# A gMLP and SwiGLU layer on one core: wd's operands prepared in quarters that share a ring with the input product, one k a step

## The chip, the cores and the metric

One Trainium2 chip, one of its cores. The metric is device time in microseconds (us) of one execution; the kernel before takes 1915.26 us, the median of three runs (1911.7 to 1916.3).

## The reference, cut to what matters

One post-norm layer on 2048 tokens of width 1024: a gated MLP mixer with spatial mixing, a layer norm, then a SwiGLU feed-forward part, with shift, scale and gate of both parts computed from a conditioning vector c. All data are float32.

```python
mod = silu(c) @ mod_w + mod_b
sh1, sc1, g1, sh2, sc2, g2 = split(mod, 6)
y = gmlp_mixer(x * (1 + sc1) + sh1)
x = layer_norm(ALPHA * x + (1 + g1) * y) * ln1_g + ln1_b
h = x * (1 + sc2) + sh2
g, u = split(h @ ffn_w_in, 2)          # 1024 -> 2 x 2816
y = (silu(g) * u) @ ffn_w_out          # 2816 -> 1024; ffn_w_out is the kernel's wd
out = layer_norm(ALPHA * x + (1 + g2) * y) * ln2_g + ln2_b
```

## The kernel before, in words

Each float32 product is three TensorE products: `parts` (line 91) splits an operand of 128 x 512 into a rounded part (a cast on ACT, line 94) and the rest (a subtraction on DVE, line 95). Both products of the feed-forward part use a Strassen-Winograd scheme: seven products of sums of blocks in place of eight. `A_OF` and `B_OF` name the operands of the seven.

The program first does the mixer for four blocks of 512 tokens (`v_part`, `us_part`, `y_part`), then `ffn_in` (line 451) twice, once for each half of the tokens (sb 0 and 1), then `ffn_out` (line 600).

`ffn_in` runs over eleven steps fp = 0..10. In a step the products stand in the order 1, 2, 5, 6, 7, 4, 3, each for the gate and the up weights (names f_<fp>g and f_<fp>u): 14 groups of 12 matmuls into the banks X, Y and Z of PSUM. `weight` (line 464) loads the four blocks of wf for product 1 (two loads of 512 KB for each of g and u), forms the sums of the later products in place on POOL (line 86), and splits each; it is called four products ahead of the matmuls. Banks are copied to SBUF tiles of the ring `c` on ACT (lines 498, 506, 513) and added to on DVE (lines 502, 514, 519); after the seven products come SiLU and product (lines 524 to 528). The seven results g, u and a21 of a step are all tiles of that ring, which has eight slots of 128 x 512. `a_operands` (line 427) forms four sums on POOL, and seven stores (line 530) bring the operands of the next product to HBM (aop).

`wd_prep(k)` (line 535) prepares wd's operands for k = 0..10: two loads of 128 x 1024 rows of wd (line 545, tiles of the ring `h3`, four slots of 128 x 1024), two multiplications by the gate g2 on DVE (line 548), four differences on DVE (line 555: T1, T3, T2, T4), and seven stores to HBM (line 540: B11, B21, B22 and the four T), which `ffn_out` reads back. g2's row comes from `spread` (line 144), called at step (5, 3) of the first half. The pieces of the eleven k are handed to the second half's steps by the table at line 768, which names steps 3 to 10 of it; `h3` serves in the same half for the loads of the half's own operands (`load_ops`, line 437). All loads and stores are issued in order on SP's queue.

The order in the source is not the order of the engines: a scheduler with a simulated clock sets the order of the instructions on each engine, and places an instruction as early as its tile's slot, its operands and its engine are free in that simulation. So the pieces of wd_prep, named for steps 3 to 10 of the second half, stand on the engines from step 0 to step 3 of it.

```python
for k, fp in enumerate((3, 4, 4, 5, 6, 6, 7, 8, 8, 9, 10)):
    for pr, step in zip((1, 2, 5, 6, 7, 4, 3), wd_prep(k)):
        later.setdefault((fp, pr), []).append(step)
```

Of the kernel before, what the change touches and what calls it, by code (L numbers as in the profile page):

```python
# [11 lines left out]
ALU = mybir.AluOpType  # L12

P = 128
# [23 lines left out]
def gmlp_swiglu_layer(  # L38
# [13 lines left out]
    nc = tc.nc  # L52
# [11 lines left out]
    ROW, HALF, UNIT = ([P, D], F32), ([P, 512], F32), ([P, 2, 512], F32R)  # L64
    cur, n = {}, [0]

    def phase(side, **tags):

        st = ExitStack()
        for tag, (bufs, kind) in tags.items():  # L70
            n[0] += 1
            p = st.enter_context(tc.tile_pool(name=f"{tag}{n[0]}", bufs=bufs, side=side, reuse_waits="tile"))
            cur[tag] = (p, kind)
        return st

    def new(tag, name, kind=None):
        p, (shape, dt) = cur[tag][0], kind or cur[tag][1]
        return p.tile(shape, dt, tag=tag, name=name)

    lo, hi = slice(0, 512), slice(512, 1024)  # L80
# [63 lines left out]
    def spread(k, name, tag="late"):  # L144

        line = dram.tile([ND, P], F32, name=f"{name}_line")
        nc.sync.dma_start(out=line.rearrange("d p -> p d"), in_=modc[:, k * ND : (k + 1) * ND])
        t = new(tag, name)
        nc.sync.dma_start(out=t, in_=line.rearrange("d p -> (d p)").partition_broadcast(P))
        return t  # L150
# [106 lines left out]
    sh1, sc1, g1, sh2, sc2, g2 = ([None] * ND for _ in range(6))  # L257
    env = {}
# [178 lines left out]
    def load_ops(sb, names):  # L437
        def tag_of(n, k):

            return "late" if n in ("A22", "S3") or (n == "S4" and k > 1) else "ops" + n  # L440

        out = {}
        for n in names:
            out[n] = []
            for k in range(NK):
                t = new("h3" if sb else "s" if n in ("S3", "A22") else "hr", f"h2{n}r_{sb}_{k}", HALF)
                nc.sync.dma_start(out=t, in_=hop[A_AT[n]][k][sb])
                out[n].append(parts(t, f"h2{n}_{sb}_{k}", tag_of(n, k)))
        return out
# [85 lines left out]
    def wd_prep(k):  # L535

        w = []

        def store(n, src):
            nc.sync.dma_start(out=wdt[n][k], in_=src)  # L540

        def load():
            for q in range(2):
                w.append(new("h3", f"wd{k}_{q}", ROW))
                nc.sync.dma_start(out=w[q], in_=wd[(2 * k + q) * P : (2 * k + q + 1) * P, :])

        def scale(q):
            nc.vector.tensor_tensor(out=w[q], in0=w[q], in1=env["g2"], op=ALU.mult)
            for n, cs in ((("B11", lo),), (("B21", lo), ("B22", hi)))[q]:
                store(n, w[q][:, cs])  # L550

        def total(n):
            b11, b12, b21, b22 = w[0][:, lo], w[0][:, hi], w[1][:, lo], w[1][:, hi]
            o, a, b = {"T1": (b11, b12, b11), "T3": (b12, b22, b12), "T2": (b22, b22, b11), "T4": (b21, b21, b22)}[n]
            nc.vector.tensor_tensor(out=o, in0=a, in1=b, op=ALU.subtract)
            store(n, o)

        return [load, lambda: scale(0), lambda: scale(1)] + [lambda n=n: total(n) for n in ("T1", "T3", "T2", "T4")]
# [153 lines left out]
    for b in range(NB):  # L712
# [35 lines left out]
    env["mix"].close()  # L748
    mix.close()
    rest = phase(  # L750
        "left", s=(4, HALF), opsS4=(2, UNIT), opsS2=(4, UNIT), h3=(4, ROW), c=(8, HALF), w=(6, UNIT), opsS1=(4, UNIT), g2=(1, ROW),
    )

    def tail(i):
        x1 = new("h3", f"x1c_{i}", ([P, NT, 2, P], F32))
        src = x1d[NB - 1].rearrange("(t p) (q k d) -> p t q k d", p=P, q=2, d=P)
        for t in range(NT):
            nc.sync.dma_start(out=x1[:, t], in_=src[:, t, :, i, :])
        h2_part(NB - 1, i, lambda t, q: x1[:, t, q, :], "h3")

    ops.update(load_ops(0, ("S1", "S2")))
    between = {(i + 2, 1): lambda i=i: tail(i) for i in range(NK)}
    between[0, 1] = lambda: (ops.update(load_ops(0, ("S3", "A22"))), norm(0), norm(1))
    between[0, 2] = lambda: (norm(2), norm(3), ops.update(load_ops(0, ("S4",))))
    between[5, 3] = lambda: env.update(g2=spread(5, "g2_bc", "g2"))

    later = {}
    for k, fp in enumerate((3, 4, 4, 5, 6, 6, 7, 8, 8, 9, 10)):
        for pr, step in zip((1, 2, 5, 6, 7, 4, 3), wd_prep(k)):
            later.setdefault((fp, pr), []).append(step)  # L770
    later = {at: lambda todo=todo: [step() for step in todo] for at, todo in later.items()}
    ffn_in(0, ops, between)
    ops = load_ops(1, ("A11", "A12", "S1", "S2", "S3", "A22", "S4"))
    ffn_in(1, ops, later)
# [52 lines left out]
```

## Time and profile before

| what | value |
|---|---|
| median of three runs | 1915.26 us (1911.7 to 1916.3) |
| the profiled execution: its time, its span | 1920.53 us, 1918.8 us |
| PE busy with matmuls | 1857.0 us, 97% of the span |
| DVE, ACT, POOL busy | 67%, 38%, 31% |
| `ffn_in`, first half and second half | about 640 to 1045 us, 1045 to 1480 us |
| `ffn_out` | about 1480 to 1919 us |
| wd_prep, first load to last store | 1047 to 1206 us |

The span is cut into steps by the matmuls: a step of `ffn_in` is the time from the start of the group f_<fp>u of product 1 to the next step's. A wait of PE is told by the profile with the instruction that ended it. The granted clock is a share of full speed: 1.00 is 2.4 GHz, and 0.50 would be 1.2 GHz.

### The profile page before, as it was taken

The numbers are of one execution on the slowest core, as the hardware profiler recorded it, in microseconds if no ns is written. First come the engines' busy times: TensorE is split into PE (matmuls) and PEld (weight loads), VectorE is DVE, ScalarE is ACT, GpSimd is POOL, SyncE is SP. The second block draws the span as 40 slices with busy tenths as digits, with TensorE's granted clock in tenths as the row PEclk, the third lists the DMA queues.
The fourth block names the chain that finished last, engine by engine and source line by source line (L and its number), as shares of the span: only waits on it lengthen the run. The fifth ranks groups of instructions, "written<-read, shape, count | busy, mean of one in ns | idle before, by whom it ended". The sixth has DMA issues, their size and how long they took to land.

```text
span 1918.8 us, 23458 instructions
## 1 busy us (share of the span) xinstructions
PE 1857.0 (97%) x8264; PEld 1534.8 (80%) x8264; DVE 1283.6 (67%) x1879; ACT 734.3 (38%) x1216; POOL 600.0 (31%) x379
## 2 busy tenths in 40 slices
PE   7999999999999999999999888999999999999997
PEld 6887788878888788888887767888888888888886
DVE  8486966786857966655568999656556344445858
ACT  3442553543445443433345223333334233333320
POOL 0000500550502656654563444356443100000104
PEclk9999999999999999999999989999999999999998
DMA  9358546564455354453227787522335655555532
GB/s 354 125 191 303 179 143 225 162 240 154 143 175 197 118 202 137 154 176 104 89 105 239 282 290 285 180 90 104 116 105 173 216 184 190 187 170 187 163 128 99
DMA packets 146151, 338.71 MB, mean 177 GB/s; under 512 B 17873, under 2 KB 22001, under 8 KB 146034
## 3 DMA queue, kind: packets, MB, share of 16 engines
q1 hardware_dynamic: 145970, 337.19, 51.4%
q8 instruction: 64, 1.05, 0.2%
q14 instruction: 53, 0.43, 0.1%
q0 software_dynamic: 64, 0.03, 0.0%
HBM read 245.14 MB, written 92.02 MB: 176 GB/s over the span
## 4 chain that ended last, share of the span: by engine, by line
PE 78%; DVE 12%; DMA 6%; issue 3%; POOL 1%; ACT 1%; SPq 0%; DVEq 0%; POOLq 0%; ACTq 0%
PE o L594 21%; PE v_ps L219 8%; PE u_ps L236 7%; PE y_ps L219 7%; PE f_5u_X L455 1%; PE f_4u_X L455 1%; PE f_8u_X L455 1%; PE f_8g_X L455 1%; PE f_7u_X L455 1%; PE f_7g_X L455 1%; PE f_6u_X L455 1%; PE f_6g_X L455 1%; PE f_5g_X L455 1%; PE f_4g_X L455 1%; PE f_3g_X L455 1%
## 5 line engine op out<-in xcount | busy, mean ns | idle before, releaser
L594 PE MATMUL o<-wd_w,alw 128*128 128x512 f32 x1848 | 419.2, 389 | 0.0
L594 PEld LDWEIGHTS o<-wd_w,alw 128*128 128x128 f32 x1848 | 347.0, 188 | 71.9
L219 PE MATMUL v_ps<-wv,hT 128*128 128x512 f32 x768 | 180.0, 396 | 16.4 <-ACT wv L94 11.9
L219 PEld LDWEIGHTS v_ps<-wv,hT 128*128 128x128 f32 x768 | 147.1, 192 | 48.4 <-ACT wv L94 12.1
L236 PE MATMUL u_ps<-hT,wu 128*128 128x512 f32 x768 | 182.6, 397 | 0.3 <-DVE v L308 0.2
L219 PE MATMUL y_ps<-wo,yT 128*128 128x512 f32 x768 | 178.0, 394 | 4.2 <-DVE sv L342 4.2
L219 PEld LDWEIGHTS y_ps<-wo,yT 128*128 128x128 f32 x768 | 145.7, 190 | 34.9 <-issue 4.5
L236 PEld LDWEIGHTS u_ps<-hT,wu 128*128 128x128 f32 x768 | 145.6, 192 | 31.2 <-issue 1.0
L95 DVE TENSOR_TENSOR alw<-al,alw 128x512 fp32r<-128x512 f32 x154 | 100.3, 686 | 87.8 <-ACT alw L94 87.8
L94 ACT CAST alw<-al 128x512 fp32r<-128x512 f32 x154 | 89.0, 620 | 140.9 <-PE o L594 136.6
L188 POOL TENSOR_TENSOR ln_rss<-ln_ves,mhalf 128x4 f32<-128x4 f32 x3 | 7.4, 2469 | 378.2 <-DVE ln_ves L187 378.2
L162 POOL TENSOR_TENSOR ln_rs<-ln_ve,mhalf 128x1 f32<-128x1 f32 x20 | 19.5, 980 | 329.4 <-DVE ln_ve L160 319.1
L95 DVE TENSOR_TENSOR wd_w<-wdl,wd_w 128x512 fp32r<-128x512 f32 x77 | 52.9, 690 | 68.7 <-ACT wd_w L94 68.7
L95 DVE TENSOR_TENSOR wu<-wu_raw,wu 128x512 fp32r<-128x512 f32 x64 | 61.2, 973 | 51.0 <-ACT wu L94 50.6
L94 ACT CAST wd_w<-wdl 128x512 fp32r<-128x512 f32 x77 | 47.7, 622 | 106.1 <-PE o L594 79.5
L94 ACT CAST wv<-wv_raw 128x512 fp32r<-128x512 f32 x64 | 37.6, 620 | 98.4 <-PE v_ps L219 42.8
L124 DVE SCALAR_TENSOR_TENSOR modw<-modw,cact 128x1024 f32<-128x1024 f32 x48 | 58.4, 1219 | 20.1 <-DMA modw<-in_modwT 20.1
L95 DVE TENSOR_TENSOR wv<-wv_raw,wv 128x512 fp32r<-128x512 f32 x64 | 47.5, 762 | 21.8 <-ACT wv L94 21.7
L95 DVE TENSOR_TENSOR wo<-wo_raw,wo 128x512 fp32r<-128x512 f32 x64 | 47.2, 748 | 20.5 <-ACT wo L94 20.5
L94 ACT CAST wo<-wo_raw 128x512 fp32r<-128x512 f32 x64 | 38.5, 616 | 43.2 <-PE y_ps L219 42.0
L94 ACT CAST wu<-wu_raw 128x512 fp32r<-128x512 f32 x64 | 38.1, 616 | 35.3 <-PE v_ps L219 18.7
L386 POOL TENSOR_TENSOR r<-r,ln1g_bc 128x1024 f32<-128x1024 f32 x16 | 42.4, 2665 | 10.0 <-ACT r L174 10.0
(611 smaller groups left out, 3776.4 us busy)
## 6 DMA issues: line engine op xcount, KB each, us to landing
al<-aop SPq DMA_DIRECT2D x154, 256.0 KB, 2.8
modw<-in_modwT SPq DMA_DIRECT2D x48, 512.0 KB, 8.3
aop<-aop_s SPq DMA_DIRECT2D x88, 256.0 KB, 2.0
wv_raw<-in_wv SPq DMA_DIRECT2D x32, 512.0 KB, 4.7
wu_raw<-in_wu SPq DMA_DIRECT2D x32, 512.0 KB, 4.2
wo_raw<-in_wo SPq DMA_DIRECT2D x32, 512.0 KB, 3.5
wd<-in_wd SPq DMA_DIRECT2D x22, 512.0 KB, 6.0
wdT<-wd SPq DMA_DIRECT2D x44, 256.0 KB, 4.7
```

The source lines that it names most:

```text
L94: nc.scalar.copy(out=o[:, 0, :], in_=src)
L95: nc.vector.tensor_tensor(out=o[:, 1, :], in0=src, in1=o[:, 0, :].bitcast(F32), op=ALU.subtract)
L124: nc.vector.scalar_tensor_tensor(out=w, in0=w, scalar=1.0, in1=env["cact"], op0=ALU.mult, op1=ALU.mult, accum_out=modc[:, j : j + 1],)
L162: nc.gpsimd.tensor_tensor(out=rs, in0=ve, in1=mhalf, op=ALU.pow)
L188: nc.gpsimd.tensor_tensor(out=rs, in0=ve, in1=mhalf.broadcast_to([P, m]), op=ALU.pow)
L219: nc.tensor.matmul(ps[t][h], lhsT=a[:, part, t * P : (t + 1) * P], rhs=w[h][:, wpart, :], start=(k == 0 and part == 0 and wpart == 0), sto ...
L236: nc.tensor.matmul(ps, lhsT=w[d // 4][:, wpart, (d % 4) * P : (d % 4 + 1) * P], rhs=rhs[d][:, part, :], start=(n == 0), stop=(n == 3 * ND ...
L386: nc.gpsimd.tensor_tensor(out=r, in0=r, in1=env["ln1g"], op=ALU.mult)
L455: nc.tensor.matmul(ps, lhsT=w[:, wpart, k * P : (k + 1) * P], rhs=a[k][:, part, :], start=(first and k == 0 and wpart == 0 and part == 0), ...
L594: nc.tensor.matmul(ps[:, cs], lhsT=a[:, part, p * P : (p + 1) * P], rhs=w[:, wpart, cs], start=(first and part == 0 and wpart == 0), stop= ...
```

## The change

wd_prep works in quarters of 128 x 512 in place of rows of 128 x 1024. The quarters are tiles of the ring `c`, which gets 11 slots in place of 8; `h3` is no longer used for them. A k has four loads of 256 KB, four multiplications, four differences and seven stores. The eleven k stand one a step, in steps 6 to 9 of the first half and 3 to 9 of the second, with one piece behind each of the seven products; steps 10, 0, 1 and 2 around the turn from one half to the other have none. g2's row is asked for at step (4, 3).

```diff
         def load():
             for q in range(2):
-                w.append(new("h3", f"wd{k}_{q}", ROW))
-                nc.sync.dma_start(out=w[q], in_=wd[(2 * k + q) * P : (2 * k + q + 1) * P, :])
+                for cs in (lo, hi):
+                    w.append(new("c", f"wd{k}_{q}{cs.start}"))
+                    nc.sync.dma_start(out=w[-1], in_=wd[(2 * k + q) * P : (2 * k + q + 1) * P, cs])
 
         def scale(q):
-            nc.vector.tensor_tensor(out=w[q], in0=w[q], in1=env["g2"], op=ALU.mult)
-            for n, cs in ((("B11", lo),), (("B21", lo), ("B22", hi)))[q]:
-                store(n, w[q][:, cs])
+            for i, cs in enumerate((lo, hi)):
+                b = w[2 * q + i]
+                nc.vector.tensor_tensor(out=b, in0=b, in1=env["g2"][:, cs], op=ALU.mult)
+                if (q, i) != (0, 1):
+                    store(("B11", None, "B21", "B22")[2 * q + i], b)
 
         def total(n):
-            b11, b12, b21, b22 = w[0][:, lo], w[0][:, hi], w[1][:, lo], w[1][:, hi]
+            b11, b12, b21, b22 = w
...
-        "left", s=(4, HALF), opsS4=(2, UNIT), opsS2=(4, UNIT), h3=(4, ROW), c=(8, HALF), w=(6, UNIT), opsS1=(4, UNIT), g2=(1, ROW),
+        "left", s=(4, HALF), opsS4=(2, UNIT), opsS2=(4, UNIT), h3=(4, ROW), c=(11, HALF), w=(6, UNIT), opsS1=(4, UNIT), g2=(1, ROW),
...
-    between[5, 3] = lambda: env.update(g2=spread(5, "g2_bc", "g2"))
+    between[4, 3] = lambda: env.update(g2=spread(5, "g2_bc", "g2"))
 
     later = {}
-    for k, fp in enumerate((3, 4, 4, 5, 6, 6, 7, 8, 8, 9, 10)):
+    for k, (sb, fp) in enumerate([(0, fp) for fp in range(6, 10)] + [(1, fp) for fp in range(3, 10)]):
         for pr, step in zip((1, 2, 5, 6, 7, 4, 3), wd_prep(k)):
-            later.setdefault((fp, pr), []).append(step)
-    later = {at: lambda todo=todo: [step() for step in todo] for at, todo in later.items()}
+            (later if sb else between)[fp, pr] = step
```

What moves on the engines is shown at three places. The first is DVE in step 0 of the second half, in the kernel before (wd is a row of wd, f_0g_w and f_0u_w are split weights, f_0g_c the result tile that line 502 adds bank Y to).

```order
1066 L548 TENSOR_TENSOR wd_0_9723<-wd_0_9723,g_bc 128x1024
1067 L95 TENSOR_TENSOR f_0g_w_8902<-f_0g_b_8843,f_0g_w_8902 128x512
1068 L548 TENSOR_TENSOR wd_1_9725<-wd_1_9725,g_bc 128x1024
1069 L95 TENSOR_TENSOR f_0u_w_8920<-f_0u_b_8850,f_0u_w_8920 128x512
1070 L548 TENSOR_TENSOR wd_0_10014<-wd_0_10014,g_bc 128x1024
1071 L502 TENSOR_TENSOR f_0g_c_8880<-f_0g_Y,f_0g_c_8880 128x512
```

The same place with the change:

```order
1097 L525 TENSOR_TENSOR f_10g_u_8665<-f_10g_u_8665,f_10u_u_8683 128x512
1098 L95 TENSOR_TENSOR f_0g_w_8994<-f_0g_b_8935,f_0g_w_8994 128x512
1099 L95 TENSOR_TENSOR f_0u_w_9012<-f_0u_b_8942,f_0u_w_9012 128x512
1100 L502 TENSOR_TENSOR f_0g_c_8972<-f_0g_Y,f_0g_c_8972 128x512
1101 L95 TENSOR_TENSOR f_0g_w_9030<-f_0g_b_8935,f_0g_w_9030 128x512
```

The three multiplications of whole rows that stood ahead of line 502 are gone; the other instructions keep their order.

The second place is DVE in step 7 of the first half, with the change (wd_00, wd_0512, wd_10 and wd_1512 are the four quarters of one k; the kernel before has the same rows there without those of lines 551 and 558).

```order
951 L95 TENSOR_TENSOR f_7u_w_7715<-f_7u_b_7571,f_7u_w_7715 128x512
952 L551 TENSOR_TENSOR wd_00_7688<-wd_00_7688,g_bc 128x512
953 L502 TENSOR_TENSOR f_7g_c_7667<-f_7g_Y,f_7g_c_7667 128x512
954 L95 TENSOR_TENSOR f_7g_w_7736<-f_7g_b_7552,f_7g_w_7736 128x512
955 L551 TENSOR_TENSOR wd_0512_7690<-wd_0512_7690,g_bc 128x512
956 L551 TENSOR_TENSOR wd_10_7692<-wd_10_7692,g_bc 128x512
957 L551 TENSOR_TENSOR wd_1512_7694<-wd_1512_7694,g_bc 128x512
958 L502 TENSOR_TENSOR f_7u_c_7686<-f_7u_Y,f_7u_c_7686 128x512
959 L558 TENSOR_TENSOR wd_00_7688<-wd_0512_7690,wd_00_7688 128x512
960 L95 TENSOR_TENSOR f_7u_w_7753<-f_7u_b_7571,f_7u_w_7753 128x512
```

The four multiplications and the first difference now stand ahead of the split of product 7's up weight (row 960); the other three differences follow within the next five rows.

The third place is SP's queue in the same step, with the change (f_8g_b and f_8u_b are the next step's loads of wf, wdB and wdT the stores of wd's operands; the kernel before has the same rows there without those of line 540).

```order
430 L468 DMA f_8g_b_7849<-in_wf 128x1024
431 L540 DMA wdB_1_316<-wd_10_7692 128x512
432 L540 DMA wdB_1_327<-wd_1512_7694 128x512
433 L540 DMA wdT_1_349<-wd_00_7688 128x512
434 L469 DMA f_8g_b_7850<-in_wf 128x1024
435 L530 DMA aop_7_0_164<-f_7g_c_7667 128x512
436 L540 DMA wdT_1_371<-wd_0512_7690 128x512
437 L540 DMA wdT_1_360<-wd_1512_7694 128x512
438 L540 DMA wdT_1_338<-wd_10_7692 128x512
439 L468 DMA f_8u_b_7868<-in_wf 128x1024
```

The second load of the next step's gate weights now stands behind three stores that wait for DVE, and the first load of its up weights behind three more.

## Rows read from the trace of the kernel before

**Rows 1.** The page, its first line.
```profile
span 1918.8 us, 23458 instructions
```

**Rows 2.** Windows over steps of ffn_in; granted clock, DMA share and GB/s end a row.
```profile
core 0: us, PE busy (x) PEld busy (x) DVE busy (x) ACT busy (x) POOL busy (x), PEclk, DMA share, GB/s
...
887.00:925.00 38.00, 38.00 (x170) 31.46 (x169) 21.44 (x25) 14.12 (x24) 18.95 (x13) 1.00 0.31 104
...
1001.10:1044.65 43.55, 39.99 (x169) 32.63 (x168) 36.89 (x46) 26.07 (x49) 14.84 (x9) 0.96 0.68 212
1044.65:1086.98 42.33, 39.15 (x170) 31.14 (x168) 37.63 (x41) 14.38 (x27) 20.41 (x12) 1.00 0.85 306
1086.98:1138.50 51.52, 43.01 (x169) 34.21 (x168) 47.50 (x51) 14.50 (x26) 22.27 (x15) 0.90 0.78 273
1138.50:1176.58 38.08, 38.08 (x169) 31.53 (x168) 34.43 (x37) 12.13 (x22) 17.83 (x11) 1.00 0.85 312
1176.58:1223.48 46.90, 41.38 (x169) 33.32 (x168) 39.73 (x44) 14.72 (x26) 25.82 (x17) 0.93 0.65 224
...
1414.00:1452.00 38.00, 38.00 (x170) 31.46 (x169) 21.45 (x25) 14.12 (x24) 18.95 (x13) 1.00 0.31 104
```

**Rows 3.** Windows over the same steps, of instructions on tile wd alone (DVE busy).
```profile
1138.50:1176.58 38.08, 18.26 (x16) 1.00 0.85 312
...
sum 222.38, DVE 74.58; mean DVE 14.92
```

**Rows 4.** Waits of PE from 1001.1 to 1223.48: total us, times, longest.
```profile
PE f_3g_X L455 <- DVE f_3g_w L95: 4.8, 1, 4.8
PE f_1g_X L455 <- DVE f_1g_w L95: 4.3, 1, 4.3
PE f_1g_Z L455 <- DVE f_1g_u L514: 4.1, 1, 4.1
PE f_10g_X L455 <- ACT f_10g_u L506: 3.6, 1, 3.6
PE f_0g_X L455 <- ACT f_0g_u L506: 1.9, 1, 1.9
PE f_0u_Z L455 <- DVE f_0u_u L514: 1.3, 1, 1.3
PE f_3u_Z L455 <- DVE f_3u_w L95: 0.7, 1, 0.7
```

**Rows 5.** Timeline of DVE in step 0 of the second half: start, us.
```profile
1054.65 2.31 DVE L548 TENSOR_TENSOR wd<-wd,g_bc 128x1024 f32<-128x1024 f32 x1
1056.88 1.77 DVE L95 TENSOR_TENSOR f_0g_w<-f_0g_b,f_0g_w 128x512 fp32r<-128x512 f32 x1
...
1062.54 0.68 DVE L502 TENSOR_TENSOR f_0g_c<-f_0g_Y,f_0g_c 128x512 f32<-128x512 f32 x1
```

**Rows 6.** Tile wd: ns min/median/max, first and last start; us to landing.
```profile
L545 SPq DMA_DIRECT2D wd<-in_wd x22: 327/382/625, 1047.3 to 1189.7; - x22
L548 DVE TENSOR_TENSOR wd<-wd,g_bc x22: 1209/1226/2311, 1054.6 to 1198.3; 128x1024 f32<-128x1024 f32 x22
...
DMA to landing us min/median/max: 2.0/4.7/8.8
```

**Rows 7.** DMA issues of the page: count, KB each, median us to landing.
```profile
aop<-aop_s SPq DMA_DIRECT2D x88, 256.0 KB, 2.0
...
wd<-in_wd SPq DMA_DIRECT2D x22, 512.0 KB, 6.0
```

**Rows 8.** Step 7 of the first half: timelines, and the chain of waits for PE.
```profile
891.77 0.32 SPq L530 DMA_DIRECT2D aop<-aop_s  x1
...
895.92 0.69 DVE L95 TENSOR_TENSOR f_7u_w<-f_7u_b,f_7u_w 128x512 fp32r<-128x512 f32 x1
...
908.78 2.72 PE f_7u_X L455 x12
...
910.86 1.29 POOL L86 TENSOR_TENSOR f_8g_b<-f_8g_b 128x512 f32<-128x512 f32 x1 [15.71 <-DVE f_8g_w L95]
```

## The prediction
> **What bounds the kernel now.** I read the windows first, cut at the steps of `ffn_in`. A quiet step has PE busy for all of its 38 us at a granted clock of 1.00, with DVE busy for 21.4 us, POOL for 19 and the DMA share at 0.31 (the first and the last of [rows 2]). PE is the bound there. A step is 14 groups of 2.72 us (the PE row of [rows 8]), that is 38.08 us. Five steps around the turn of the halves stand out: step 10 of the first half and steps 0 to 3 of the second take 43.55, 42.33, 51.52, 38.08 and 46.90 us [rows 2]. Their sum is 222.38 us [rows 3] against 5 x 38.08 = 190.40, so 32.0 us are lost: 5.5, 4.25, 13.4, 0 and 8.8.
>
> Next come PE's waits in that stretch [rows 4]. Seven waits make 20.7 us. The other 11.3 us are groups that PE ran slowly after a wait: its busy time in the five steps adds to 201.6 us, 11.2 over 190.4, and the granted clock there is 0.96, 1.00, 0.90, 1.00 and 0.93 [rows 2], a mixture of full speed (2.4 GHz) and its half. A wait therefore costs about half as much again behind it.
>
> Whose waits are they? Wd's pieces run on DVE from 1054.6 us, and the first load is issued at 1047.3 [rows 6]. The wait in step 10 ended before 1044.65, so **it is not wd's**, and 5.5 us of the 32.0 lie outside this change. In steps 0, 1 and 3 the matmuls wait for DVE's splits and additions (lines 95, 514), or for ACT that stands behind DVE. In those steps DVE is busy for 37.63, 47.50 and 39.73 us, more than PE's 38.08 in two of them, or within half a microsecond of it. Of its busy time in the four steps 74.58 us are on tile wd [rows 3]. The timeline shows how it works: a multiplication of a whole row takes 2.31 us, and three such stand ahead of line 502's addition of step 0, which runs only at 1062.54 [rows 5].
>
> **The change part by part.**
>
> *Removed at the turn.* All of wd's DVE work, loads and stores leave steps 0 to 3 of the second half up to step 3, and the order of what stays is as it was. Step 0 without it: 37.63 less a share of 74.58 leaves DVE some 19 us below PE's time. Its wait for line 506 goes, since what held ACT was line 502 behind the three rows, some 5.8 us (2.31 twice and 1.21, the median of line 548 being 1.226 [rows 5, 6]). I take steps 0, 1 and 3 back to 38.08: **4.25 + 13.4 + 8.8 = 26.5 us**. The other work of the turn, the split of the second half's own operands, still falls into step 10 and the start of step 0, so I keep 1.0 us of the 1.3 us that the group f_0u_Z waited [rows 4]: **25.5 us**.
>
> *Added to eleven quiet steps.* A k has eight DVE operations of 128 x 512. Such an operation takes 0.69 us with POOL idle [rows 8] and 1.77 with POOL running beside it [rows 5]. So a step gets 5.5 us at best and 14.2 at worst, and DVE goes from 21.4 to 26.9 or 35.6 us of 38.08. Both lie below what step 2 of the second half had: 18.26 us of wd's work, DVE busy for 34.43 in all, and PE without a gap [rows 2, 3]. POOL rests for 15.71 us up to 910.86, which is where the order puts most of the eight [rows 8], so I take 5.5 to 8 us, and zero on PE.
>
> *The waiting instruction and what stands behind it.* In order on DVE, the first quarter's multiplication stands ahead of line 502's addition, the next three ahead of the split of product 7's up weight. That split runs at 895.92 now and PE's group that uses it starts at 908.78 [rows 8]: 12.2 us to spare after its 0.69. The last quarters' loads are issued behind the store at 891.77. With 2 to 3 us to landing they arrive near 895.5; the three multiplications, line 502, T1 and then the split take 6 x 0.69 = 4.1 us, and the split ends near 900, 3 us later than now and 9 us before its use. The three differences behind it add 2 us to the following splits, whose groups come 2.72 us apart behind that one. Cost: zero, and the cover is those 9 us.
>
> *SP's queue.* Four loads and seven stores join each of the eleven steps. The next step's second gate load stands behind three stores that wait for DVE (until about 899). It is needed in the next step's product 2, seven groups behind the one at 908.78, so near 927.8: no cost. The up loads go out later than the last T store anyway. Bytes: 2.8 MB in 38 us add 75 GB/s to 104, and 312 GB/s went through step 2 without a loss [rows 2].
>
> *The ring.* Eleven tiles a step on eleven slots: a slot comes round after one step. A quarter's slot is free when its last store has landed, near 905; its successor is loaded a step after 891.77, near 930. Cost zero.
>
> *g2's row.* The two DMAs of `spread` keep their place in SP's order. Zero.
>
> *Smaller transfers.* A row of 512 KB took a median of 6.0 us to land at the crowded turn, and stores of 256 KB take 2.0 in quieter steps [rows 7]. The load's time is not in the sum, since a quarter has 12 us of cover; its bounds are 2.0 and the 8.8 us of the slowest wd transfer [rows 6].
>
> The Trainium skill, "DMA: Bandwidth & Descriptors", under "Measured (HBM→SBUF, 128 partitions, SWDGE, issued from GpSimd)", speaks against this part: batch transfers to 1 MiB or more. By its fit under "Anatomy of one DMA" (2.0 us and the bytes at 436 GB/s), 22 loads of 512 KB are an estimated 70 us and 44 of 256 KB 114 us; the 44 us between them would, all on the path, make the kernel slower by some 18 us. The DMA share of 0.31 in the quiet steps says that they have room beside PE.
>
> **The sum.** The profiled execution took 1920.53 us for its span of 1918.8 [rows 1]; less 25.5 that is 1895.0. It lies 5.3 us above the median of the runs, 1915.26; from the median I get 1889.8, rounded to **1890 us**. The measurement of this kernel tells about 0.3% (5.7 us) from no change.
>
> **The rivals.**
>
> 1. *The turn keeps its own jam.* DVE reaches step 0 already late: line 519 and the splits of the second half's operands fill it there. If that, and not wd, made the waits of step 0, and half of those in step 1, then 4.25 + 6.7 us stay and the gain is 15.5: 1900 us. For it: DVE is busy for 36.89 us in step 10, where wd has no work [rows 2]. Against it: the three whole rows ahead of line 502.
> 2. *A small toll on each of eleven steps.* If a piece comes late by half a microsecond to one in each, 5.5 to 11 us come back: 1895 to 1901 us. For it: eight in-order operations between those that PE awaits. Against it: step 2 paid nothing for twice as many.
> 3. *The quarters' loads land late, slower than before.* DVE stands at a quarter's multiplication, and the split of product 7's up weight stands behind it. From 892.5 the load would have to take more than 12 us for PE to wait; then each step pays like step 3's wait, 4.8 us [rows 4], and 11 x 4.8 = 53 against 26.5 gives 1942 us. With the slowest 8.8 us of rows 6 the split ends near 905, 3 us early. It decides only beyond 12 us. The rule on batches of 1 MiB (the Trainium skill, "DMA: Bandwidth & Descriptors", as above) points to this rival; no row here shows a transfer that slow.
> 4. *The scheduler pulls the pieces together again*, and nothing changes: 1915 us. The order excludes it almost: four k stand in the first half, one a step.
> 5. *Step 10's loss goes too*: 32.0 us, 1883 us. Nothing of the change is there.
>
> **How the numbers follow.** Forecast 0.68, the turn's own jam 0.13, the small toll 0.10, late quarters 0.04, no change 0.03, the larger gain 0.02. The rest of the forecast's own spread is some 3 us of run to run. The range takes in the first three: 1883 to 1903 us. Faster by over 0.3% means below 1909.5: the forecast, the larger gain, and the first two rivals nearly whole, 0.90. Within 0.3%: 0.05. Slower: 0.05.
>
> **What would show it.** In the profile after, windows of 38.1 us for steps 0 to 3 of the second half, with at most 1 to 2 us over in step 0, and step 10 near 43.5 as before. Steps 6 to 9 of the first half and 3 to 9 of the second at 38.1 with DVE at 27 to 30 us, no wait of PE in them, and the granted clock at 1.00. Line 551 twice as often as line 548 and half as long. A wait of PE on a split (line 95) that comes back once a step would prove me wrong through rivals 2 or 3; a DVE wait on a quarter's load ahead of it tells the third. Waits of PE in steps 0 and 1 with DVE full and no wd in sight would show the first rival.

## The result and the profile after

The changed kernel took 1894.38 us (median of four executions, 1890.18 to 1895.16) beside 1915.78 of the kernel before (1911.7 to 1920.65): a ratio of 0.9883, 95% interval 0.9855 to 0.991 (the two medians alone give 0.9888). Timed again later it took 1889.13 beside 1917.42: 0.9854, 0.9835 to 0.9873. The forecast was 1890 us, 1883 to 1903.

The page of the changed kernel, its first lines (busy time of an engine, its share of the span, instructions); the span answers to [rows 1]:

```profile
span 1888.5 us, 23484 instructions
## 1 busy us (share of the span) xinstructions
PE 1844.8 (98%) x8264; PEld 1528.4 (81%) x8264; DVE 1278.1 (68%) x1901; ACT 736.3 (39%) x1216; POOL 595.1 (32%) x379
```

DVE does as much as before, in more instructions; what became shorter is PE's time. The windows of the changed kernel, cut at the same steps as [rows 2]: step 7 of the first half, steps 10, 0, 1, 2 and 3 around the turn, and one late step of the second half (after the step's length: busy us of PE, PEld, DVE, ACT, POOL, then the granted clock, DMA share and GB/s).

```profile
885.55:923.60 38.05, 38.05 (x169) 31.50 (x169) 27.17 (x33) 14.11 (x24) 18.99 (x13) 1.00 0.52 180
...
999.77:1041.33 41.56, 38.40 (x170) 31.46 (x169) 35.41 (x44) 24.88 (x46) 14.69 (x9) 1.00 0.68 220
1041.33:1079.41 38.08, 38.08 (x169) 31.53 (x169) 30.98 (x34) 17.18 (x31) 24.46 (x16) 1.00 0.38 133
1079.41:1117.49 38.08, 38.08 (x169) 31.53 (x169) 21.51 (x25) 14.11 (x24) 19.02 (x13) 1.00 0.33 111
1117.49:1155.57 38.08, 38.08 (x169) 31.53 (x169) 21.52 (x25) 14.12 (x24) 19.02 (x13) 1.00 0.34 111
1155.57:1193.64 38.07, 38.07 (x169) 31.52 (x169) 26.16 (x33) 14.00 (x24) 18.55 (x13) 1.00 0.55 186
...
1383.90:1422.00 38.10, 38.10 (x170) 31.55 (x169) 27.22 (x33) 14.11 (x24) 19.04 (x13) 1.00 0.52 179
```

Steps 0, 1 and 3 of the second half, which took 42.33, 51.52 and 46.90 us, take 38.08, the length of a step whose matmuls never wait. That is 26.5 us. Step 10 of the first half takes 41.56 in place of 43.55. Together 28.5 of the 30.3 us between the two spans lie in these steps; the remaining 1.8 lie ahead of them and behind, in work that the change does not touch. A step with one k has DVE at 26 to 27 us and the granted clock at 1.00.

PE's waits from 640 to 1500 us in the changed kernel (total us, times, longest): of the seven in [rows 4] one is left, that of step 10. The other three lie in step 1 of the first half, in both kernels.

```profile
PE f_10g_X L455 <- ACT f_10g_u L506: 3.2, 1, 3.2
PE f_1u_Y L455 <- DVE f_1u_w L95: 3.1, 1, 3.1
PE f_1g_Y L455 <- ACT f_1g_w L94: 1.3, 1, 1.3
PE f_1g_Y L455 <- DVE f_1g_w L95: 0.9, 1, 0.9
```

The windows of tile wd alone in the changed kernel, for three steps that have one k (DVE busy, with its operations), answer to [rows 3]:

```profile
885.55:923.60 38.05, 6.07 (x8) 1.00 0.52 180
1155.57:1193.64 38.07, 5.58 (x8) 1.00 0.55 186
1383.90:1422.00 38.10, 6.14 (x8) 1.00 0.52 179
```

And all uses of tile wd (ns of one: least, median, most; first and last start; then what DVE waited for ahead of wd's operations, in us and times; last the us from issue to landing, of wd's loads and stores together; the loads alone took 3.0, 4.1 and 5.0), which answer to [rows 6]:

```profile
L546 SPq DMA_DIRECT2D wd<-in_wd x44: 423/430/1382, 849.7 to 1390.1; - x44
L551 DVE TENSOR_TENSOR wd<-wd,g_bc x44: 683/693/1673, 852.9 to 1395.4; 128x512 f32<-128x512 f32 x44
...
  DMA wd<-in_wd: 12.3, 19
  DMA wdB<-wd: 8.0, 10
...
DMA to landing us min/median/max: 2.7/4.1/6.3
```

The eight operations of a k cost DVE about 6 us in all. DVE does stand at them, 12.3 us in total for quarters that have not landed and 8.0 us for stores that still read a quarter, and PE feels none of it. The cover is visible in DVE's timeline in step 7, against [rows 8] (start and length in us):

```profile
894.60 1.93 DVE L551 TENSOR_TENSOR wd<-wd,g_bc 128x512 f32<-128x512 f32 x3 [0.38 <-DMA wd<-in_wd]
896.45 0.68 DVE L502 TENSOR_TENSOR f_7u_c<-f_7u_Y,f_7u_c 128x512 f32<-128x512 f32 x1
...
897.65 0.69 DVE L95 TENSOR_TENSOR f_7u_w<-f_7u_b,f_7u_w 128x512 fp32r<-128x512 f32 x1
```

The split of product 7's up weight begins at 897.65 here. This step starts 1.47 us earlier than before (885.55 against 887.02), so the split has slipped by 3.2 us, and 9 us are left before its matmuls.

### The profile page after: what moved, and what is told of

Same layout as the page of the kernel before. It is cut to its first block, busy times and chain, and to the rows that moved or that the text cites. A ratio compares the mean times of both kernels' runs of the same rounds, so it can differ in the third digit from the quotient of the medians.

```text
span 1888.5 us, 23484 instructions
## 1 busy us (share of the span) xinstructions
PE 1844.8 (98%) x8264; PEld 1528.4 (81%) x8264; DVE 1278.1 (68%) x1901; ACT 736.3 (39%) x1216; POOL 595.1 (32%) x379
## 4 chain that ended last, share of the span: by engine, by line
PE 85%; DVE 10%; DMA 3%; issue 1%; ACT 1%; SPq 0%; DVEq 0%; ACTq 0%
PE o L597 21%; PE u_ps L236 7%; PE y_ps L219 7%; PE v_ps L219 5%; DVE modw L124 2%; PE f_5u_X L455 1%; PE f_4u_X L455 1%; PE f_3u_X L455 1%; PE f_2u_X L455 1%; PE f_9g_X L455 1%; PE f_9u_X L455 1%; PE f_8u_X L455 1%; PE f_7u_X L455 1%; PE f_7g_X L455 1%; PE f_6u_X L455 1%; PE f_6g_X L455 1%
## 5 line engine op out<-in xcount | busy, mean ns | idle before, releaser
L551 DVE TENSOR_TENSOR wd<-wd,g_bc 128x512 f32<-128x512 f32 x44 | 36.9, 861 | 12.7 <-DMA wd<-in_wd 12.3
```

The lines of the kernel that those rows point to most:

```text
L551: nc.vector.tensor_tensor(out=b, in0=b, in1=env["g2"][:, cs], op=ALU.mult)
```

## The experiments

The theory: wd's operations, bunched on DVE, held up the splits and additions that PE waits for; spread over steps with room they cost nothing. The rivals: SP's queue and the crowded transfers made the waits, not DVE; the place (the turn) is what hurts and not the bunching; the eleven steps pay a small toll that the spread of the runs hides. Of the change's parts, the table may bring the gain, or the quarters in the ring. One execution of this kernel differs from the next by several us (the changed kernel: 1885.7 to 1895.2 over eight), so most verdicts rest on the steps of the profile, which repeat to hundredths.

**The preparation left out.**

```diff
-    for k, (sb, fp) in enumerate([(0, fp) for fp in range(6, 10)] + [(1, fp) for fp in range(3, 10)]):
-        for pr, step in zip((1, 2, 5, 6, 7, 4, 3), wd_prep(k)):
-            (later if sb else between)[fp, pr] = step
...
-        nc.sync.dma_start(out=t, in_=wdt[B_OF[pr]][k])
+        nc.sync.dma_start(out=t, in_=wd[2 * k * P : (2 * k + 1) * P, lo])
```

> The changed kernel without wd's preparation: no loads, multiplications, differences or stores of it, and the last product reads rows of the unscaled wd in its operands' place, so that part of the result is left out. If the eleven steps pay nothing for the preparation, the time is that of the changed kernel, 1890 to 1895 us, and each of the steps 6 to 9 and 3 to 9 stays at 38.08 us. If every step pays a toll of 0.5 to 1 us that hides in the spread of the runs, it is 5 to 11 us faster: 1880 to 1889.

Measured: 1887.07 us, and every step from 6 to 9 and from 0 to 9 at 38.08 us, exactly as with the preparation. Its step 10 took 43.23. The total alone would have fitted the toll; the steps rule it out. In these steps the preparation of wd is free now.

**DVE's work left out of the kernel before.**

```diff
-            nc.vector.tensor_tensor(out=w[q], in0=w[q], in1=env["g2"], op=ALU.mult)
...
-            nc.vector.tensor_tensor(out=o, in0=a, in1=b, op=ALU.subtract)
```

> The kernel before without wd's work on DVE (22 multiplications and 44 differences are left out, so wd's operands are wrong); its loads and stores stay, at the turn of the halves. If DVE's queue made the waits, steps 0, 1 and 3 of the second half lose at most 1 to 3 us of their 26.5, and the time is 1889 to 1896 us. If SP's queue or the crowded transfers made them, the steps still lose 15 us or more: 1904 to 1916.

Measured: 1892.9 us. The windows of its steps 10, 0, 1, 2 and 3:

```profile
1000.73:1043.65 42.92, 40.02 (x170) 32.60 (x168) 36.54 (x46) 25.81 (x48) 14.86 (x9) 0.96 0.66 215
1043.65:1081.73 38.08, 38.08 (x170) 31.53 (x168) 25.30 (x29) 14.83 (x27) 19.24 (x13) 1.00 0.96 355
1081.73:1119.81 38.08, 38.08 (x170) 31.53 (x168) 24.14 (x28) 14.85 (x26) 21.02 (x14) 1.00 1.04 395
1119.81:1157.89 38.08, 38.08 (x170) 31.53 (x168) 22.23 (x26) 13.89 (x24) 21.24 (x15) 1.00 0.99 373
1157.89:1195.97 38.08, 38.08 (x170) 31.53 (x168) 21.40 (x25) 14.01 (x24) 19.02 (x13) 1.00 0.50 173
```

All loads and stores of wd are still there, denser than before (DMA share 0.96 to 1.04, up to 395 GB/s for a whole step), and no step from 0 to 3 waits. So the waits came through wd's instructions on DVE; the crowded transfers do not make them by themselves. This run takes away two things at once, though: the time that wd's instructions need, and the time that DVE stands at one of them for its load (the stores, too, no longer wait for DVE). That the second had a part is seen in the kernel before, in step 0 (start and length in us; in brackets the idle time just before, and what ended it):

```profile
1079.93 1.23 DVE L548 TENSOR_TENSOR wd<-wd,g_bc 128x1024 f32<-128x1024 f32 x1 [4.63 <-DMA wd<-in_wd]
1081.08 0.68 DVE L514 TENSOR_TENSOR f_0u_u<-f_0u_Z,f_0u_u 128x512 f32<-128x512 f32 x1
```

DVE did nothing for 4.63 us because a row of wd had not landed. Right behind stands the addition for which PE waited 1.3 us (f_0u_Z in [rows 4]). Ahead of the two longest waits, of f_3g_X and f_1g_X, DVE was at work without a gap. How much of the 26.5 us belongs to either part was not separated.

**One k a step, but at the turn.**

```diff
-    for k, (sb, fp) in enumerate([(0, fp) for fp in range(6, 10)] + [(1, fp) for fp in range(3, 10)]):
+    for k in range(NP):
         for pr, step in zip((1, 2, 5, 6, 7, 4, 3), wd_prep(k)):
-            (later if sb else between)[fp, pr] = step
+            later[k, pr] = step
```

> The changed kernel with its quarters and its ring, but the eleven k in steps 0 to 10 of the second half, one a step, so that three meet the turn. If the rate counts (how much of wd's work falls into a step), step 0 has DVE at 31.0 + 6 = 37 us of 38.08 and loses 0 to 2 us, steps 1 and 2 nothing: 1890 to 1897 us. If the turn itself is what hurts, step 0 loses its 4.25 us again and step 1 some of its 13.4: 1897 to 1910.

Measured: 1890.9 us, its steps 0 and 1, and PE's wait in step 0:

```profile
1037.14:1079.98 42.84, 40.34 (x170) 32.52 (x168) 35.59 (x43) 17.51 (x32) 23.19 (x15) 0.96 0.56 185
1079.98:1118.06 38.08, 38.08 (x170) 31.53 (x168) 26.39 (x33) 14.02 (x24) 20.14 (x14) 1.00 0.57 193
```

```profile
PE f_0g_X L455 <- ACT f_0g_u L506: 2.5, 1, 2.5
```

One k in step 0 costs 4.8 us, more than the bunch cost there before (4.25), and in steps 1 and 2 nothing. So both the place and the rate count, each in its step: the 22.3 us of steps 1 and 3 came from the bunching, and step 0 is a worse place for one k than the other steps. It has less room, since DVE has 31 us of its own there, but DVE is not full (35.59 of 42.84 us). It stood 1.91 us at wd's first multiplication for a quarter's load, and line 502's addition came behind that:

```profile
1054.49 1.33 DVE L551 TENSOR_TENSOR wd<-wd,g_bc 128x512 f32<-128x512 f32 x2 [1.91 <-DMA wd<-in_wd]
1055.73 0.68 DVE L502 TENSOR_TENSOR f_0g_c<-f_0g_Y,f_0g_c 128x512 f32<-128x512 f32 x1
```

ACT waited 5.0 us for this addition, with line 506's copy, for which PE waited, further back in its order. How much of the 4.8 us is the load's and how much the multiplications' was not separated. My expectation for the rate was too low for step 0. The total of the run would not have shown it.

**The table alone, with rows in h3.**

```diff
-    between[5, 3] = lambda: env.update(g2=spread(5, "g2_bc", "g2"))
+    between[4, 3] = lambda: env.update(g2=spread(5, "g2_bc", "g2"))
...
-    for k, fp in enumerate((3, 4, 4, 5, 6, 6, 7, 8, 8, 9, 10)):
+    for k, (sb, fp) in enumerate([(0, fp) for fp in range(6, 10)] + [(1, fp) for fp in range(3, 10)]):
         for pr, step in zip((1, 2, 5, 6, 7, 4, 3), wd_prep(k)):
-            later.setdefault((fp, pr), []).append(step)
-    later = {at: lambda todo=todo: [step() for step in todo] for at, todo in later.items()}
+            (later if sb else between)[fp, pr] = step
```

> The kernel before with rows of 128 x 1024 in h3, and only the table of the change (steps 6 to 9 and 3 to 9, one k a step). On SP's queue the scheduler puts 28 of the pieces behind the loads issued in step 6 of the first half, 6 behind those of step 7, and 10, 28 and 25 behind those of steps 0, 1 and 2 of the second half. If the rate counts, the first half loses too, some 5 to 13 us around steps 6 and 7 where no turn is, and steps 0 to 2 of the second half lose 10 to 22: 1905 to 1925 us. If the turn alone hurts, the first half loses nothing and the time is 1895 to 1905. If the table were what brought the gain, it is 1890 to 1895.

Measured: 1915.31 us, no gain. The windows of steps 5 and 6 of the first half, and of steps 0 and 1 of the second; then the larger of PE's waits:

```profile
805.26:848.15 42.89, 40.87 (x177) 33.42 (x176) 33.77 (x32) 13.99 (x24) 21.07 (x13) 0.96 0.76 277
848.15:889.78 41.63, 39.33 (x170) 31.23 (x168) 37.71 (x42) 14.22 (x26) 23.27 (x15) 1.00 0.70 246
...
1045.48:1089.92 44.44, 40.97 (x169) 32.28 (x168) 39.49 (x44) 16.20 (x30) 20.37 (x12) 0.96 0.83 296
1089.92:1142.12 52.20, 43.20 (x170) 34.40 (x168) 47.20 (x51) 14.51 (x26) 21.98 (x15) 0.87 0.77 268
```

```profile
PE f_1g_Z L455 <- DVE f_1g_u L514: 4.6, 1, 4.6
PE f_1g_X L455 <- DVE f_1g_w L95: 4.3, 1, 4.3
...
PE f_5g_Z L455 <- DVE f_5g_u L514: 2.0, 1, 2.0
```

The table names one k a step, but the scheduler places rows as early as h3's four slots come free, so they bunch again: 3.9 us are lost in step 5 (38.97 without), 3.6 in step 6, where no turn is, and 20.5 in steps 0 and 1 of the second half. Ahead of the addition that PE waited for in step 5 (the last row above) DVE again stood for a load:

```profile
834.11 1.23 DVE L548 TENSOR_TENSOR wd<-wd,g_bc 128x1024 f32<-128x1024 f32 x1 [2.62 <-DMA wd<-in_wd]
835.25 0.68 DVE L514 TENSOR_TENSOR f_5g_u<-f_5g_Z,f_5g_u 128x512 f32<-128x512 f32 x1
```

**The quarters and the ring, with the table of before.**

```diff
-    for k, (sb, fp) in enumerate([(0, fp) for fp in range(6, 10)] + [(1, fp) for fp in range(3, 10)]):
+    for k, fp in enumerate((3, 4, 4, 5, 6, 6, 7, 8, 8, 9, 10)):
         for pr, step in zip((1, 2, 5, 6, 7, 4, 3), wd_prep(k)):
-            (later if sb else between)[fp, pr] = step
+            later.setdefault((fp, pr), []).append(step)
+    later = {at: lambda todo=todo: [step() for step in todo] for at, todo in later.items()}
```

> The changed kernel's quarters and ring of eleven slots with the table of before, which puts two k into steps 4, 6 and 8 of the second half and one into 3, 5, 7, 9 and 10. The ring ties a piece to its step, so none stands in steps 0 to 2. If the ring's tie is what brought the gain, steps 0 to 2 stay at 38.08 us, a step with two k has DVE at 21.5 + 12 = 33.5 us and loses nothing, and the time is 1890 to 1895 us. If more than one k a step costs, steps 4, 6 and 8 lose 2 to 8 us each: 1896 to 1915.

Measured: 1887.65 us. All steps from 0 to 9 take 38.08 us, and those with two k too; one of them, step 4, with DVE at 30.85:

```profile
1190.69:1228.77 38.08, 38.08 (x169) 31.56 (x168) 30.85 (x41) 14.00 (x24) 19.05 (x13) 1.00 0.73 256
```

It was timed again beside the changed kernel:

> The quarters and the ring with the table of before. If the ring alone brings the gain, its ratio to the kernel before is that of the changed kernel within 0.2%.

> The changed kernel again, for a narrower interval and for the spread of step 10 and of the mixer: steps 0 to 3 at 38.08 us, 20 to 27 us below the kernel before.

Measured: 1890.82 us, ratio 0.9865 (0.9846 to 0.9884), beside the changed kernel's 0.9854 (0.9835 to 0.9873); each ratio lies within the other's interval. The quarters in the ring bring the gain, with either table. Quarters and ring stand together in every run; quarters in `h3` were not tried, so what each of the two gives is open. What they do together is seen in where wd's operations ran in the first of these runs, in steps 2 and 4 (DVE busy on tile wd, with its operations):

```profile
1114.53:1152.61 38.08, 0.00 (x0) 1.00 0.33 111
1190.69:1228.77 38.08, 11.35 (x16) 1.00 0.73 256
```

No operation of wd runs in steps 0 to 2, and steps 3 to 10 have 8 or 16 each, just as the table names them, while rows in `h3` by the same table ran in steps 0 to 3. The reason that I give, that a tile of the ring waits for the tiles of the running step ahead of it and so no piece can be placed before its step, fits this and was not tried by itself.

**Wd's work on DVE doubled and tripled.** For three times (for twice, range(2) and range(1)):

```diff
-                nc.vector.tensor_tensor(out=b, in0=b, in1=env["g2"][:, cs], op=ALU.mult)
+                for _ in range(3):
+                    nc.vector.tensor_tensor(out=b, in0=b, in1=env["g2"][:, cs], op=ALU.mult)
...
             nc.vector.tensor_tensor(out=o, in0=a, in1=b, op=ALU.subtract)
+            for _ in range(2):
+                nc.vector.tensor_tensor(out=o, in0=o, in1=env["g2"][:, lo], op=ALU.mult)
```

> The changed kernel with every operation of wd on DVE done twice (16 in place of 8 a step; wd's values are then other than the reference's). DVE would be busy for about 27.2 + 5.9 = 33 us of a step's 38.08. By the slack read in the prediction (the split of product 7's up weight 9 us before its use, 4 more operations of 0.69 ahead of it) the steps stay at 38.08 and the time at 1890 to 1895 us. If the eleven steps are near their edge, each loses 1 us or more: 1901 and up.

> The changed kernel with every operation of wd on DVE done three times (24 a step; wd's values are other than the reference's). DVE would need about 27.2 + 11.8 = 39 us of a step's 38.08. If DVE's total in a step is the limit, each of the eleven steps grows to 39 to 41 us and the time to 1900 to 1925. If only single deadlines count and DVE has room elsewhere, the steps stay at 38.08.

Measured: 1885.0 us doubled and 1904.1 tripled. First a window of the doubled one (step 5 of the second half):

```profile
1226.32:1264.39 38.07, 38.07 (x169) 31.54 (x168) 31.97 (x41) 14.11 (x24) 19.03 (x13) 1.00 0.54 180
```

Then of the tripled one, steps 8 and 10 of the first half and step 5 of the second, and one of its waits:

```profile
918.51:957.74 39.23, 38.38 (x169) 31.47 (x168) 37.26 (x48) 13.23 (x24) 19.08 (x13) 1.00 0.51 173
...
997.57:1045.76 48.19, 40.73 (x169) 33.16 (x168) 39.28 (x49) 27.08 (x50) 18.98 (x12) 0.89 0.61 203
1236.73:1276.55 39.82, 38.42 (x170) 31.46 (x168) 37.84 (x49) 13.39 (x24) 19.67 (x13) 1.00 0.53 172
```

```profile
PE f_9g_Z L455 <- DVE f_9g_u L514: 2.9, 2, 1.5
```

Sixteen operations a step are free; 24 take 18.5 us, DVE is busy for 37.84 of 39.82 us, and a step grows by 1.74. So the changed kernel has a margin of at least one more such set per step, and its end is near DVE's total. That each of the eleven steps grows was wrong: steps 6 and 7 of the first half and 3 of the second stay at 38.08, and step 4 grows by 0.57, so a backlog has to build up first. Step 10, behind steps 8 and 9, lost 10 us in place of 3 to 5, which I read as their backlog.

**Two attempts at what is left in step 10.** ACT stands at a cast of S1's operands there, which waits for the load, and line 506's copy stands behind it. First, two operands to a slot of h3:

```diff
-                t = new("h3" if sb else "s" if n in ("S3", "A22") else "hr", f"h2{n}r_{sb}_{k}", HALF)
+                if not sb:
+                    t = new("s" if n in ("S3", "A22") else "hr", f"h2{n}r_{sb}_{k}", HALF)
+                elif k % 2 == 0:
+                    pair = new("h3", f"h2{n}r_{sb}_{k}", ROW)
+                    t = pair[:, lo]
+                else:
+                    t = pair[:, hi]
```

> The changed kernel, and besides it the second half's own operands loaded two to a slot of h3 (128 x 1024), which wd no longer uses, so that eight and not four of them are under way or wait at the turn. Step 10 of the first half loses 3.5 to 5.4 us now, because ACT stands at a cast for the load of S1's operands with line 506 behind it. If the four slots make those loads late, step 10 falls to 38 to 40 us and the time to 1886 to 1893 us. If the splits on DVE and ACT are what is late, step 10 stays at 41 to 43.5 us, or steps 10 and 0 grow.

Measured: 1892.01 us; step 10 took 44.48. S1's operands came in time, but the scheduler then put casts of S3 ahead of line 506's next copy (line 512 in that kernel), and the wait went there. The first row is PE's, the second ACT's:

```profile
PE f_10u_X L461 <- ACT f_10u_u L512: 3.3, 1, 3.3
```

```profile
ACT h2S L94 <- DMA h2S3r<-hop: 4.4, 1, 4.4
```

Then the casts of S1 and S2 on POOL:

```diff
+        if pool:
+            nc.gpsimd.tensor_copy(out=o[:, 0, :], in_=src)
+        else:
+            nc.scalar.copy(out=o[:, 0, :], in_=src)
...
-                out[n].append(parts(t, f"h2{n}_{sb}_{k}", tag_of(n, k)))
+                out[n].append(parts(t, f"h2{n}_{sb}_{k}", tag_of(n, k), bool(sb) and n in ("S1", "S2")))
```

> The changed kernel with the eight casts of S1 and S2 of the second half on POOL, which rests for 22.9 us in step 10, in place of ACT, where they stand ahead of line 506's copies. If ACT's order behind a late load makes step 10's loss, it falls from 41 to 43 us to 38.1 to 39.5, the time by about 3 us. If POOL's casts slow DVE's splits beside them more than ACT's freedom gives back, step 10 or step 0 grows by 1 us or more.

> The changed kernel with the casts of S1 and S2 on POOL, again and timed. Steps 10 and 0 together took 78.84 us in its first look and 79.63 to 81.07 in the three looks at the ring with casts on ACT, so I expect it 0.8 to 2 us below the changed kernel, at a ratio of 0.984 to 0.986 to the kernel before, which does not tell it from the changed kernel by time alone.

Measured: 1884.69 us in one execution, then a median of 1887.35 (ratio 0.9866, 0.9847 to 0.9886). The windows of steps 10 and 0 in the second of these runs, and PE's longest wait there:

```profile
995.00:1033.08 38.08, 38.08 (x170) 31.54 (x169) 32.85 (x38) 17.82 (x32) 21.51 (x17) 1.00 0.60 203
1033.08:1075.29 42.21, 39.27 (x170) 31.24 (x168) 34.46 (x40) 20.04 (x36) 24.11 (x16) 1.00 0.47 154
```

```profile
PE f_0g_X L458 <- DVE f_0g_w L98: 1.6, 1, 1.6
```

Step 10 lost nothing for the first time, so ACT's order behind a late load made its loss. Step 0 gave it back, by 2.7 and 4.1 us, with PE now waiting for DVE. Steps 10 and 0 together took 78.84 and 80.29 us, against 79.64 and 79.84 in two runs of the changed kernel: a moved wait, and no version that can be told from the changed kernel by its time.

## Why the prediction was right

- *The 26.5 us of steps 0, 1 and 3* are what came back, to a hundredth per step, by the path named: without wd's instructions on DVE the kernel before has those steps at 38.08. The prediction counted only the time that these instructions take; in part DVE lost its time standing at them for their loads, which leave the turn with them.
- *The 1.0 us kept for step 0* was not there: step 0 is 38.08, or 38.10 in the second profile. The prediction put the wait of f_0u_Z down to the splits of the second half's operands; DVE's 4.63 us stand for a load of wd came right ahead of it.
- *The room in step 0* was read too large: DVE was to be some 19 us below PE's time there and is 7 below (30.98 us of 38.08). Since the change puts nothing into step 0, it cost nothing.
- *Step 10 was to stay near 43.5.* It took 41.0 to 43.0 us in six runs with the ring (41.56 in the profile shown; the tripled run and the two attempts at step 10 left aside), and 43.23 without wd. It varies from one execution to the next and is no part of the change; in the profiled pair it happened to add 2.0 us to the gain.
- *Zero on PE in eleven steps* held. The term was 5.5 to 8 us of DVE a step, and 5.6 to 6.1 were measured. The split of product 7's up weight slipped by 3.2 us, forecast as 3.
- *The landing of a quarter* was mis-sized: 2 to 3 us assumed, a median of 4.1 and at most 5.0 measured for the loads. The cover of 12 us made it harmless: there are twice as many loads of half the size, and DVE's waits for them, 12.3 us in all, never reached PE. The Trainium skill, "DMA: Bandwidth & Descriptors", under "Measured (HBM→SBUF, 128 partitions, SWDGE, issued from GpSimd)", says to batch transfers to 1 MiB or more. That rule did not decide the time here.
- *Rival 1, the turn's own jam:* it caused none of the loss, but step 0 is a worse place for one k, which costs 4.8 us there. *Rival 2, a toll:* none. *Rival 3, late quarters:* not in the change as made; with one k in step 0 a quarter came 1.9 us late ahead of an addition that PE's wait hangs on.
- *Rival 4, that the pieces are pulled together again,* is what happens to the table without the ring. The order excluded it for the change as made; it shows that the table is not the part that does the work.

The sum was 25.5 us. The medians of the two timings differ by 21.4 and 28.3, and the steps say 26.5 and what step 10 does in that execution. That 25.5 lies between the two timings is in part luck, since the 1.0 us taken off was wrong. The rest of the spread stays open in part: it lies in step 10, in step 1 of the first half (49.8 us in the changed kernel, 50.9 before) and ahead of the feed-forward part, and was not traced further.

## What to carry to other kernels

Where a scheduler places work as early as its slots allow, a table of steps is a wish; the ring that the tiles share held it in this kernel. To spread a side job, let it draw its slots from the ring of the main job's own step. And judge a spread not by the engine's total alone: wd's 18 us in step 2 of the kernel before cost nothing, and 14.6 in step 5 with the new table and rows cost 3.9, because there a multiplication that stood 2.6 us for its load came ahead of an addition that PE awaited. What counts on an engine that works in order is what stands behind the side job's instructions, and what these wait for themselves.

## What the runs showed of the hardware that was not expected

- A whole step with the DMA share at 1.04 and 395 GB/s (the kernel before without wd's work on DVE) left PE at a granted clock of 1.00 and without a wait, though the weights of the next step came through the same queue.
- What a wait in step 10 costs behind it does not follow from its length. PE waited 3.6 us in the kernel before and 2.9 in the one without wd's work on DVE, and both had a granted clock of 0.96 over the step and some 40.0 us of PE's time for 38.1 us of work; after 3.2 us in the changed kernel and 3.4 in the one with one k a step at the turn the clock was 1.00 and PE's time 38.4. So a wait of 3 us costs 3 us or 5; what decides was not tried.
